# A transformer step on one core: softmax scaling and decay rows moved to other engines and queues, and a value product moved to a later stage

## The chip, the cores and the metric

The kernel runs on one core of a Trainium2 chip, as one program, once per measurement. The metric is device microseconds of one execution. TensorE (PE) does the matrix products, VectorE (DVE), ScalarE (ACT) and GpSimd (POOL) the elementwise work, and SyncE (SP) issues most of the transfers between memory and the on-chip buffers.

## The reference

One pre-norm block (a mixer with sparse attention, a cross-attention to a memory of 256 rows, a gated feed-forward part), followed by two hybrid layers. All of it is float32, with 512 positions and width 1024. The parts that the change touches:

```python
# cross-attention of the first block
kv = rmsnorm(mem, norm_mem_kv) @ w_kv_mem           # (256, 1024): keys, values
p = softmax(q @ k.T * 128 ** -0.5);  o = p @ v      # 4 heads of 128

# one of the two hybrid layers
q, k, v, z_attn, z_ssm, xbc, dt_raw = split(x @ w_in)
attn = window_attention(q, k, v, sinks) * silu(z_attn)      # 16 heads of 64, 4 key heads
xs, bm, cm = split(silu(conv4(xbc)))
dt = softplus(dt_raw + dt_bias)
a_cs = cumsum(dt * -exp(a_log))                             # inside each chunk of 128
cb = cm @ bm.T                                              # per chunk and group
y = (cb * exp(a_cs[l] - a_cs[s]) masked to s <= l) @ (xs * dt)   # 16 heads of 64
y = y + (cm @ state) * exp(a_cs) + xs * d_skip              # state carried over the chunks
ssm = rmsnorm_by_group(y * silu(z_ssm)) * ssm_norm_w
x = layer_norm(alpha * x + concat(attn, ssm) @ w_out)
```

## The kernel before

Every product with weights is made from halves: a weight tile of 128x1024 float32 is loaded (`wraw`), ScalarE casts it to a rounded half `whi`, VectorE subtracts to get `wlo` (function `weights`, three buffers of each kind), and activations are split in the same way into a pair. A product of 512 columns is then 24 matmuls of one projection: 16 with `whi` (lines L147, L148) and 8 with `wlo` (L152).

Five kinds of stage follow each other: `mem_kv` (products of the memory, and the norm of the input, in two halves A and B of 256 positions), `mixer`, `memory`, `ffn`, and twice `hybrid`. In `hybrid` the convolutions come first, then the loop over eight pairs of SSM heads, then the projections of keys (two tiles, `W[0]`, `W[1]`) and values (`W[2]`, `W[3]`), the gated norm of the second half of the heads, and the attention over (tile, key head) units, whose first work is `queries(0)`.

For a pair of heads, `decay` makes two 128x512 tiles of weights: a matmul with a selecting vector spreads a row of a_cs over the partitions (L1041), ScalarE takes Relu of the difference in four pieces (L1045) and exponents (L1047, L1048), and the tile is multiplied with `cb` (L1049), on VectorE for one head and on GpSimd for the other. `heads` uses them as operands (L1061, L1067) and VectorE combines (L1069, L1070, L1071, L1098). In the attention, VectorE and ScalarE make a softmax (L1160 to L1167), L1169 scales it, for two of four parts on GpSimd, and L1183 transposes it on TensorE.

The order on TensorE, VectorE, ScalarE and GpSimd is set by the framework's scheduler when the program is built, and each engine then works through its list in order. SP's list is the order in which the code issues, because the program asks for that:

```python
ctx.enter_context(tc.manual_schedule(engines={mybir.EngineType.SP}))
```

## Time and profile before

| | |
|---|---|
| time, median of 3 runs | 1673.09 us (1672.94 to 1673.29) |
| the profiled execution | 1672.5 us |
| its span, first to last instruction | 1670.7 us (1.8 us of the time lie around it) |
| mean granted TensorE clock over the span | 0.993 |
| busy: PE, DVE, ACT, POOL | 1621.6, 1115.1, 838.0, 239.2 us |
| share of the span | 97%, 67%, 50%, 14% |

TensorE is busy nearly all the time. A share over the whole span does not tell what ends a wait in one stage; the rows further below are taken by stage for that reason.

### The profile page before, as it was taken

Reading aid. Unit: us, or ns where it says so; the run is one execution under the profiler, and the core shown is the slowest. Engines: PE = TensorE matmul, PEld = TensorE weight load, DVE = VectorE, ACT = ScalarE, POOL = GpSimd, SP = SyncE. Lnnn points to the kernel's source line nnn. Section 1 sums busy time; section 2 is a strip of 40 time slices with the busy share of each in tenths; the row PEclk is TensorE's granted clock in tenths of the full one; section 3 lists DMA queues with packets and bytes.
Section 4 is the critical chain, followed back from the end, with each engine's and each line's share of the span. In section 5 each row is a group of like instructions: output and inputs, shape, how many; then the busy total and the mean of one; then the engine's idle time right before and its main releaser. Section 6 shows DMA issues by size and latency. Waiting matters only on the chain.

```text
span 1670.7 us, 24187 instructions
## 1 busy us (share of the span) xinstructions
PE 1621.6 (97%) x9046; PEld 1362.4 (82%) x9046; DVE 1115.1 (67%) x2199; ACT 838.0 (50%) x1648; POOL 239.2 (14%) x267
## 2 busy tenths in 40 slices
PE   8999999999999999999999999999999999999996
PEld 5778888889888888889988677777998867777786
DVE  6779866548885545523677888765487788866447
ACT  4443255336763233223554776664355477766424
POOL 2010113010200000000000223221230023222121
PEclk9999999999999999999999999999999999999998
DMA  6522322143143233234632122111452211212133
GB/s 223 196 96 76 119 96 76 64 151 119 62 150 104 89 101 101 87 102 129 212 93 89 38 64 89 64 64 56 141 177 82 79 38 57 96 61 65 66 103 112
DMA packets 57719, 166.50 MB, mean 100 GB/s; under 512 B 6673, under 2 KB 15841, under 8 KB 57601
## 3 DMA queue, kind: packets, MB, share of 16 engines
q1 hardware_dynamic: 49216, 155.21, 29.0%
q10 hardware_dynamic: 8384, 9.73, 1.8%
q8 instruction: 71, 1.16, 0.3%
q14 instruction: 48, 0.39, 0.1%
HBM read 158.61 MB, written 8.93 MB: 100 GB/s over the span
## 4 chain that ended last, share of the span: by engine, by line
PE 78%; DVE 11%; ACT 5%; issue 2%; POOL 2%; DMA 1%; SPq 0%; ACTq 0%; DVEq 0%; POOLq 0%
PE psmm L148 21%; PE psmm L152 21%; PE psmm L147 21%; DVE wlo L108 2%; POOL w L1169 2%; PE psmm L175 2%; PE psmm L173 2%; PE psmm L174 2%; ACT w L1164 1%; DVE w L1160 1%; DVE G L130 1%; PE pstr L1061 1%; PE pstr L1183 1%; PE pslg L561 1%; PE pslg L1020 1%
## 5 line engine op out<-in xcount | busy, mean ns | idle before, releaser
L147 PE MATMUL psmm<-G,whi 128*128 128x512 f32 (+1 forms) x1196 | 468.5, 393 | 1.3 <-ACT whi L107 1.3
L148 PE MATMUL psmm<-G,whi 128*128 128x512 f32 (+1 forms) x1196 | 464.3, 389 | 0.0
L108 DVE TENSOR_TENSOR wlo<-wraw,whi 128x1024 fp32r<-128x1024 f32 (+3 forms) x265 | 320.4, 1210 | 184.8 <-ACT whi L107 99.2
L107 ACT CAST whi<-wraw 128x1024 fp32r<-128x1024 f32 (+3 forms) x265 | 270.9, 1025 | 340.3 <-PE psmm L148 291.3
L152 PE MATMUL psmm<-G,wlo 128*128 128x512 f32 (+1 forms) x1196 | 296.3, 388 | 0.0
L148 PEld LDWEIGHTS psmm<-G,whi 128*128 128x128 f32 x1196 | 225.3, 188 | 47.2 <-issue 4.2
L147 PEld LDWEIGHTS psmm<-G,whi 128*128 128x128 f32 x1196 | 225.3, 188 | 47.2 <-issue 2.4
L152 PEld LDWEIGHTS psmm<-G,wlo 128*128 128x128 f32 x1196 | 222.7, 189 | 46.4 <-issue 1.5
L148 PE MATMUL psmm<-R,whi 128*128 128x256 f32 (+1 forms) x732 | 222.7, 326 | 0.0
L147 PE MATMUL psmm<-R,whi 128*128 128x256 f32 (+1 forms) x732 | 222.6, 326 | 0.0
L147 PEld LDWEIGHTS psmm<-R,whi 128*128 128x128 f32 x732 | 139.2, 190 | 11.8 <-issue 0.3
L148 PEld LDWEIGHTS psmm<-R,whi 128*128 128x128 f32 x732 | 139.2, 190 | 11.5
L152 PE MATMUL psmm<-R,wlo 128*128 128x256 f32 (+1 forms) x732 | 138.1, 326 | 0.0
L152 PEld LDWEIGHTS psmm<-R,wlo 128*128 128x128 f32 x732 | 112.8, 190 | 11.5
L198 POOL TENSOR_TENSOR acc<-acc,sq 128x512 f32<-128x512 f32 (+1 forms) x42 | 53.4, 1272 | 454.4 <-ACT sq L197 454.4
L1164 ACT ACTIVATE w<-w,st 128x256 f32<-128x256 f32 (+1 forms) x128 | 60.2, 471 | 33.5 <-DVE st L1162 33.2
L1169 POOL TENSOR_SCALAR w<-w,st 128x256 f32<-128x256 f32 x64 | 46.1, 730 | 134.6 <-DVE st L1167 127.0
L209 ACT ACTIVATE sq<-ht 128x512 f32<-128x512 f32 (+1 forms) x48 | 29.4, 613 | 58.5 <-DVE ht L907 29.3
L1049 POOL TENSOR_TENSOR R<-R,R 128x512 f32<-128x512 f32 x16 | 21.7, 1353 | 228.3 <-ACT R L1048 228.3
L907 DVE SCALAR_TENSOR_TENSOR ht<-psmm,cwh,ht 128x511 f32<-128x511 f32 (+2 forms) x72 | 53.5, 743 | 1.2
L837 DVE TENSOR_TENSOR sq<-psmm,G 128x512 f32<-128x512 f32 (+1 forms) x24 | 15.5, 645 | 57.3 <-PE psmm L152 57.3
L566 POOL TENSOR_TENSOR G<-G,G 128x384 f32<-128x384 f32 (+2 forms) x24 | 28.9, 1217 | 162.1 <-DMA G<-ts 93.4
(348 smaller groups left out, 2701.8 us busy)
## 6 DMA issues: line engine op xcount, KB each, us to landing
wraw<-w_in SPq DMA_DIRECT2D x112, 512.0 KB, 3.4
wraw<-w_out SPq DMA_DIRECT2D x56, 512.0 KB, 3.8
wraw<-w_down SPq DMA_DIRECT2D x24, 512.0 KB, 3.5
wraw<-w_gate SPq DMA_DIRECT2D x22, 512.0 KB, 3.3
wraw<-w_up SPq DMA_DIRECT2D x22, 512.0 KB, 3.3
wraw<-w_down SPq DMA_DIRECT2D x12, 384.0 KB, 3.2
wraw<-w_proj_attn SPq DMA_DIRECT2D x8, 512.0 KB, 3.4
ts<-t SPq DMA_DIRECT2D x4, 640.0 KB, 7.0
```

The costliest lines, as they stand in the source:

```text
L107: nc.scalar.copy(hi[:, :n], raw[:, :n])
L108: nc.vector.tensor_tensor(lo[:, :n], raw[:, :n], hi[:, :n].bitcast(F32), ALU.subtract)
L147: nc.tensor.matmul(out, whi[:, c], xh, start=start and k == 0, stop=False)
L148: nc.tensor.matmul(out, whi[:, c], xl, start=False, stop=False)
L152: nc.tensor.matmul(out, wlo[:, c], xh, start=False, stop=stop and k == n - 1)
L173: nc.tensor.matmul(o, whi[:, cc], xh[:, c], start=k == 0 and i % 2 == 0, stop=False, skip_group_check=True)
L174: nc.tensor.matmul(o, whi[:, cc], xl[:, c], start=False, stop=False, skip_group_check=True)
L175: nc.tensor.matmul(o, wlo[:, cc], xh[:, c], start=False, stop=k == n - 1, skip_group_check=True)
L198: (eng or nc.gpsimd).tensor_tensor(acc, acc, t, ALU.add)
L907: nc.vector.scalar_tensor_tensor(y[:, s:], pt[:, : S - s], cw(3 - s), y[:, s:], ALU.mult, ALU.add)
L1164: nc.scalar.activation(prs[b], prs[b], AF.Exp, bias=nm[:, b : b + 1], accum_out=sm[:, b : b + 1])
L1169: (nc.gpsimd if b % 2 else nc.vector).tensor_scalar(prs[b], prs[b], rc[:, b : b + 1], 1.0, ALU.mult, ALU.mult)
```

## The change

Stage 1 no longer makes the value product of the memory; the normed-by-weight memory `mgd` goes out to memory, and the stage `memory` loads it and makes the 16 products there. The memory's squares go from GpSimd to ScalarE. The first weights of `mixer` are loaded before the second half's norm. In `memory` all softmax scaling is on VectorE, the stores of `xd` go from ACT's to SP's queue, and the first three weight tiles of the next stage are split there. In `hybrid` the selecting matmuls (32 in both layers) are gone: a_cs and its exponent are written out by two transfers of ACT, and SP reads their rows back spread over the partitions (64 transfers of rows of 512 and of 384 columns). One head of a pair gets its difference on VectorE (L1045 of after, 64 pieces in both layers), the other stays on ScalarE. All products with `cb` and all softmax scaling are on VectorE. The projections of values and keys move into turns 5, 6 and 7 of the loop, and the copies of the keys' other half, eight per layer, go from GpSimd to SP. Line numbers below L133 of before shift by up to 15 in after.

```diff
     def mem_kv(self):
-        def square(k):
-            t = self.f("R")[:, :256]
-            nc.gpsimd.tensor_tensor(t if k else acc, ms[k], ms[k], ALU.mult)
-            if k:
-                nc.gpsimd.tensor_tensor(acc, acc, t, ALU.add)
...
+        for j, t in enumerate(mgs):
+            nc.sync.dma_start(self.mgd[j], t)
+        for k in range(KD):
+            self.sumsq(half(ms[k // 2])[k % 2], acc, k == 0, nc.vector)
...
-        for c in range(4):
-            w = raw(a["w_v_mem"][c])
-            for kk in range(2):
-                k = 2 * c + kk
-                for t in range(2):
-                    nc.tensor.matmul(pts[t], mg[k][:, t * P : (t + 1) * P], w[:, 512 * kk : 512 * kk + 512], start=k == 0, stop=k == 7)
...
     def memory(self):
+        def memory_values():
+            pts = [self.ps() for _ in range(2)]
+            for k in range(KD):
+                m, w = mgs[k // 2], wv[k // 2][:, S * (k % 2) : S * (k % 2) + S]
+                for t, pt in enumerate(pts):
+                    o = 256 * (k % 2) + P * t
+                    nc.tensor.matmul(pt, m[:, o : o + P], w, start=k == 0, stop=k == 7)
...
-                (nc.vector if i else nc.gpsimd).tensor_scalar(p, p, rc[:, i : i + 1], 1.0, ALU.mult, ALU.mult)
+                nc.vector.tensor_scalar(p, p, rc[:, i : i + 1], 1.0, ALU.mult, ALU.mult)
...
     def hybrid(self, L):
-        self.split(acs, ahl[0:16, :], ahl[32:48, :])
+        nc.scalar.dma_start(self.acsd[0], acs)
+        nc.scalar.activation(seg, acs, AF.Exp)
+        nc.scalar.dma_start(self.acsd[1], seg)
...
+        def decay_rows(j):
+            dfs, ee = [self.f("R") for _ in range(2)], self.f("R")
+            for e_, df in enumerate(dfs):
+                row = self.acsd[:, 2 * j + e_, :]
+                nc.sync.dma_start(df, row[:1].broadcast_to([P, S]))
+                nc.sync.dma_start(ee[64 * e_ : 64 * e_ + 64, P:], row[1:, P:].broadcast_to([64, S - P]))
+            return dfs, ee
...
         def decay(j):
+            dfs, ee = rows.pop(0)
+            if j < 6:
+                rows.append(decay_rows(j + 2))
...
-                nc.tensor.matmul(pb, self.sel[:, hd : hd + 1].broadcast_to([48, P]), ahl, start=True, stop=True)
...
-                nc.scalar.activation(ee[rows, P:], pb[rows, P:], AF.Exp)
-                nc.scalar.activation(df, df, AF.Exp, scale=-1.0)
-                (nc.vector if e_ else nc.gpsimd).tensor_tensor(df, df, cb[hd // 8], ALU.mult)
+                    if e_:
+                        nc.scalar.activation(df[:, cc], df[:, cc], AF.Relu, bias=at, scale=-1.0)
+                    else:
+                        nc.vector.tensor_scalar(df[:, cc], df[:, cc], at, 0.0, ALU.subtract, ALU.min)
+                nc.scalar.activation(df, df, AF.Exp, scale=-1.0 if e_ else 1.0)
+                nc.vector.tensor_tensor(df, df, cb[hd // 8], ALU.mult)
...
+        def keys(j):
+            pt = self.proj(W[j], h)
...
+                for t in (kh, kl):
+                    nc.sync.dma_start(t[o].bitcast(F32), t[r].bitcast(F32))
+            return ks
...
+            elif j == 5:
+                vs = token_values()
+            else:
+                kt.append(keys(j - 6))
...
-                for t in (kh, kl):
-                    nc.gpsimd.tensor_copy(t[o], t[r].bitcast(F32))
...
-                (nc.gpsimd if b % 2 else nc.vector).tensor_scalar(prs[b], prs[b], rc[:, b : b + 1], 1.0, ALU.mult, ALU.mult)
+                nc.vector.tensor_scalar(prs[b], prs[b], rc[:, b : b + 1], 1.0, ALU.mult, ALU.mult)
```

On SP, at the end of the first layer's SSM heads, before has nothing but loads of weight tiles (the third row here is the first tile of queries):

```order
L104 DMA wraw_9343<-w_in 128x1024
L104 DMA wraw_9397<-w_in 128x1024
L104 DMA wraw_9487<-w_in 128x1024
L104 DMA wraw_9557<-w_in 128x1024
L104 DMA wraw_9640<-w_in 128x1024
```

The same place in the change: 9124 and 9178 are the value tiles, 9266 is the first key tile, 9376 the second, 9473 and 9544 the first two of queries, and `G` are the halves of the split keys.

```order
L105 DMA wraw_9266<-w_in 128x1024
L1089 DMA G_9297<-G_9297 64x512
L1089 DMA G_9298<-G_9298 64x512
L1089 DMA G_9299<-G_9299 64x512
L1089 DMA G_9300<-G_9300 64x512
L105 DMA wraw_9376<-w_in 128x1024
L1089 DMA G_9407<-G_9407 64x512
L1089 DMA G_9408<-G_9408 64x512
L1089 DMA G_9409<-G_9409 64x512
L1089 DMA G_9410<-G_9410 64x512
L105 DMA wraw_9473<-w_in 128x1024
L105 DMA wraw_9544<-w_in 128x1024
```

Four copies of a key tile's halves, which need that tile's product split, now stand ahead of the load of the next tile's weights.

On TensorE, after the first key tile's product (`psmm_9272`) the change has seven matmuls of the last pair of heads (the first two and the last are shown), the sum of the gated norm's squares (L207), and the product of the second key tile (`psmm_9382`):

```order
L155 MATMUL psmm_9272<-G_6645,wlo_9269 128x512
L1058 MATMUL pstr_9419<-R_9083,G_8985 64x128
L1058 MATMUL pstr_9419<-R_9082,G_8998 64x128
...
L1058 MATMUL pstr_9419<-R_9083,G_9026 64x128
L207 MATMUL pstr_9440<-acc_9118,ones 128x512
L150 MATMUL psmm_9382<-G_6631,whi_9376 128x512
```

In before the products of both key tiles and the values stand ahead of that sum, and the queries' product follows it at once; now one key tile's product stands behind it, and the queries' (`psmm_9480`) follow that with nothing between.

On VectorE, in the first pairs of heads, before has one product with `cb` per pair (L1049, tile `R`), here beside a convolution (L907, L910) and the combining of a pair:

```order
L1070 TENSOR_TENSOR R_8649<-R_8649,pstr_8759 128x384
L1049 TENSOR_TENSOR R_8662<-R_8662,R_8397 128x512
L907 SCALAR_TENSOR_TENSOR ht_8689<-psmm_8697,cwh_7787,ht_8689 128x511
L1069 SCALAR_TENSOR_TENSOR G_8353<-G_8353,vecs,pstr_8750 128x512
L907 SCALAR_TENSOR_TENSOR ht_8689<-psmm_8697,cwh_7787,ht_8689 128x510
L1071 TENSOR_TENSOR G_8353<-G_8353,R_8649 128x384
```

The change has there, with the difference in pieces (L1045) and two products (L1047) per pair:

```order
L1045 TENSOR_SCALAR R_8684<-R_8684,dtt_8304 128x128
L1133 TENSOR_TENSOR G_8315<-G_8315,R_7825 128x512
L1045 TENSOR_SCALAR R_8684<-R_8684,dtt_8304 128x128 x3
L1047 TENSOR_TENSOR R_8685<-R_8685,R_8399 128x512
L1045 TENSOR_SCALAR R_8743<-R_8743,dtt_8304 128x128 x4
L111 TENSOR_TENSOR wlo_8785<-wraw_8782,whi_8784 128x1024
L1047 TENSOR_TENSOR R_8684<-R_8684,R_8399 128x512
L1047 TENSOR_TENSOR R_8743<-R_8743,R_8399 128x512
```

Four pieces and a second product per pair of heads are added to VectorE's list between the combining of one pair and the weights of the next projection.

## Rows read from the trace of the kernel before

**Rows 1.** Busy time of each engine in stretches of the span, in us.

```profile
core 0: us, PE busy (x) PEld busy (x) DVE busy (x) ACT busy (x) POOL busy (x), PEclk, DMA share, GB/s
0.00:20.00 20.00, 13.73 (x52) 10.75 (x53) 11.36 (x23) 4.82 (x10) 11.23 (x20) 1.00 0.92 304
399.60:494.40 94.80, 87.85 (x671) 83.95 (x672) 78.18 (x198) 66.38 (x172) 10.25 (x14) 0.96 0.25 84
920.90:991.80 70.90, 69.66 (x376) 49.08 (x375) 60.11 (x85) 54.55 (x124) 16.38 (x12) 1.00 0.17 53
1030.00:1154.20 124.20, 120.81 (x698) 97.25 (x697) 85.83 (x254) 80.29 (x219) 28.90 (x46) 1.00 0.19 61
```

**Rows 2.** What TensorE waited for: line, releaser, total us, times, longest.

```profile
PE pstr L1183 <- POOL w L1169: 5.7, 14, 0.6
PE pslg L1154 <- DVE G L130: 5.0, 2, 2.5
PE pstr L204 <- DVE acc L198: 4.4, 2, 3.4
```

**Rows 3.** The value product of the memory in stage 1, by line and shape.

```profile
L710 PE MATMUL pslg<-wraw,R 128*128 128x512 f32 x32 | 14.5, 595 | 0.0
```

**Rows 4.** TensorE in order of time, at four places of the first layer.

```profile
931.00 0.49 PE L1041 MATMUL pslg<-ahl,selr 48*128 48x512 f32 x1
931.43 0.50 PE L152 MATMUL psmm<-G,wlo 128*128 128x512 f32 x1
...
1012.97 0.28 PE L1127 MATMUL psmm<-whi,G 128*128 128x256 f32 x1
1013.09 0.28 PE L1128 MATMUL psmm<-wlo,G 128*128 128x256 f32 x1
...
1020.13 0.39 PE L147 MATMUL psmm<-G,whi 128*128 128x512 f32 x1
1020.35 0.39 PE L148 MATMUL psmm<-G,whi 128*128 128x512 f32 x1
...
1025.08 0.33 PE L1154 MATMUL pslg<-G,G 128*128 128x128 f32 x1 [2.52 <-DVE G L130]
```

**Rows 5.** VectorE's groups by shape, 932.9 to 1024.8 us.

```profile
L1098 DVE TENSOR_TENSOR G<-G,R 128x512 f32<-128x512 f32 x8 | 8.4, 1056 | 0.1
L1071 DVE TENSOR_TENSOR G<-G,R 128x384 f32<-128x384 f32 x8 | 6.8, 846 | 0.1
```

**Rows 6.** VectorE in order of time, first layer.

```profile
938.67 0.69 DVE L1098 TENSOR_TENSOR G<-G,R 128x512 f32<-128x512 f32 x1
...
1022.49 1.22 DVE L108 TENSOR_TENSOR wlo<-wraw,whi 128x1024 fp32r<-128x1024 f32 x1
...
1024.34 0.68 DVE L130 TENSOR_TENSOR G<-psmm,G 64x512 fp32r<-64x512 f32 x1
```

**Rows 7.** VectorE's nearest kind to the new pieces, whole span, by shape.

```profile
L453 DVE TENSOR_SCALAR G<-G,st 128x128 f32<-128x128 f32 x8 | 2.2, 281 | 0.0
```

**Rows 8.** GpSimd's products with `cb`, 932.9 to 1024.8 us.

```profile
L1049 POOL TENSOR_TENSOR R<-R,R 128x512 f32<-128x512 f32 x7 | 9.4, 1341 | 33.7 <-ACT R L1048 33.7
```

**Rows 9.** ScalarE in order of time, end of the first layer's heads.

```profile
1015.08 1.28 ACT L220 ACT_TABLE_LOAD   x1
...
1019.58 1.04 ACT L107 CAST whi<-wraw 128x1024 fp32r<-128x1024 f32 x1
...
1022.46 0.57 ACT L129 CAST G<-psmm 64x512 fp32r<-64x512 f32 x1
```

**Rows 10.** SP's loads of a layer's weights: KB each, median us from issue to landing.

```profile
wraw<-w_in SPq DMA_DIRECT2D x112, 512.0 KB, 3.4
```

**Rows 11.** What SP's queue waited for: total us, times, longest.

```profile
SPq L104 <- DVE wlo L108: 1241.9, 218, 30.9
```

**Rows 12.** The stretches behind TensorE's two longest waits; PEclk is the granted clock.

```profile
466.40:473.20 6.80, 6.26 (x24) 5.47 (x25) 5.20 (x9) 5.14 (x9) 0.00 (x0) 0.51 0.51 147
1026.10:1029.50 3.40, 3.40 (x11) 2.68 (x10) 3.34 (x9) 2.18 (x3) 0.00 (x0) 0.54 0.09 36
```

More of the change, by code (lines that the diff above doesn't have):

```diff
@@ L457, in mixer @@
         h = self.h
-        W = iter(range(32))
+        W = iter(range(2, 32))
         unit = lambda: self.proj(a["w_in"][next(W)], h)
-        first = [(self.ps(), 68, self.weights(a["w_idx"], 8 * 68))]
-        first += [(self.ps(), P, self.weights(a["w_in"][next(W)])) for _ in range(2)]
+        first = [(self.ps(), m, w) for m, w in self.first]
         for c in self.HALVES:
@@ L672, in mem_kv @@
         for k in range(KD):
-            t = self.f("R")[:, :256]
-            nc.vector.tensor_scalar(t, ms[k], self.col("norm_mem_kv", k), None, ALU.mult)
+            m, t = half(ms[k // 2])[k % 2], half(mgs[k // 2])[k % 2]
+            nc.vector.tensor_scalar(t, m, self.col("norm_mem_kv", k), None, ALU.mult)
             mg.append(t)
-            square(k)
+        banks = [self.ps("lg") for _ in range(2)]
+        pks = [t for bank in banks for t in half(bank)]
         for j in range(4):
-            if j == 3:
-                wk.append(raw(a["w_k_mem"][3]))
-                self.consts2()
-            pt = self.ps()[:, :256]
-            pks.append(pt)
             for k in range(KD):
-                nc.tensor.matmul(pt, wk[j][:, k * P : k * P + P], mg[k], start=k == 0, stop=k == 7)
-        self.bias_tables()
+                nc.tensor.matmul(pks[j], wk[j][:, k * P : k * P + P], mg[k], start=k == 0 and j % 2 == 0, stop=k == 7,
+                                 skip_group_check=True)
         self.h = self.pairs("G")
@@ L689, in mem_kv @@
         self.pump()
+        self.first = [(68, self.weights(a["w_idx"], 8 * 68))] + [(P, self.weights(a["w_in"][j])) for j in range(2)]
+        self.consts2()
+        for j, t in enumerate(mgs):
+            nc.sync.dma_start(self.mgd[j], t)
+        for k in range(KD):
+            self.sumsq(half(ms[k // 2])[k % 2], acc, k == 0, nc.vector)
         self.rstd(rs, acc, 1e-6)
-        rt = self.s("rt", (P, 4), 2)[:, :2]
+        self.rtm = self.s("rtm", (P, 2))
         pr = self.ps("tr")
@@ L694, in mem_kv @@
             nc.tensor.matmul(pr[:, t : t + 1], acc[:, t * P : (t + 1) * P], self.ones[:, :1], start=True, stop=True)
-        self.inv_sqrt(rt, pr[:, :2], self.s("ru", (P, 2), 2), 1e-6)
-        def key(j):
+        self.inv_sqrt(self.rtm, pr[:, :2], self.s("ru", (P, 2), 2), 1e-6)
+        self.pending = norm(B)
+        self.pump(1)
+        for j in range(4):
             t = self.f("ht")[:, :256]
@@ L809, in memory @@
                 pb.append(logits(j, B))
+        self.ahead = [self.weights(z) for z in (a["w_gate"][0], a["w_up"][0], a["w_gate"][1])]
         for j in range(4):
@@ L844, in ffn @@
         g = [self.f("ht") for _ in range(2)]
-        first = [self.weights(z) for z in (a["w_gate"][0], a["w_up"][0], a["w_gate"][1])]
-        first.append(self.held(a["w_up"][1], "R"))
+        first = self.ahead + [self.held(a["w_up"][1], "R")]
         for c in self.HALVES:
@@ L1207, in queries @@
             return qs
+        self.piece = S
         q = queries(0)
```

152 lines of the change are left out of this document (67 added, 85 removed).

## The prediction, made before the changed kernel was run

> **What bounds the kernel now.** I read the shares by stretch first. TensorE is the bound nearly everywhere: in the first layer's SSM heads it works 69.7 of 70.9 us, and VectorE 60.1 of the same 70.9 [rows 1]. So VectorE has about 11 us of room there, no more. Then the list of waits: in the attention it is GpSimd's half of the softmax scaling that ends 14 short waits, 5.7 us in both layers; where a layer passes from heads to attention, the split of the first queries ends a wait of 2.5 us, twice; and a sum of squares ends one of 3.4 us in the memory stage [rows 2]. Behind two such gaps the clock is lower: after the 3.4 us gap, 6.8 us at 0.51 of full speed, after the 2.5 us gap, 3.4 us at 0.54 [rows 12], which is the 1.2 GHz level instead of 2.4, so that about half of each stretch is lost. The first 20 us hold 6.3 us without TensorE work [rows 1].
>
> **Stage 1 and the memory stage.** Stage 1 loses 32 records of the value product, 14.5 us busy [rows 3]. That work stands in a stage with idle TensorE time, ahead of the second half's norm. What VectorE and ScalarE do for this norm stays, and they now also square the memory. So not all of it is gained: at most about 11 us, at least 3, if the norm is what ends last. I take 6.5, a little under half of the 14.5, since I see nothing left that TensorE could do in the wait for that norm. The same product costs its 14.5 us in the memory stage, but that stage has 94.8 − 87.9 = 6.9 us without TensorE work and a lower clock after its longest gap, worth 3.4 us [rows 1, 12]. The product's matmuls stand among the logits and the next stage's first three weight tiles are split early, so most of these 10.3 us can be covered. Cost: between 14.5 − 10.3 = +4.2 and +8 if the gap at the sum of squares stays whole; below, +1 if the order saves switches as well. I take +4. The xd transfers that go to SP's list stand ahead of loads that are needed later than they arrive; I cost them at nothing, hidden by the 94.8 us stage, and up to 2 us if that cover is gone.
>
> **Heads: VectorE's list.** Per layer 16 selecting matmuls go. One takes 0.43 us from its start to the next matmul's [rows 4], and the switches around it some more, so about 8 us of TensorE work. But VectorE gains work in the same stretch: 32 pieces of 128x128, 0.28 each by the nearest row [rows 7], and eight products, 0.69 each by a row of the same shape [rows 6]. That is 14.5 us by durations; neighbours overlap a little, so I take 12 (bounds 10 and 14.5). What it gets back is GpSimd's disturbance: L1098 takes 1.06 on the mean and 0.69 undisturbed, eight times, and L1071 0.85 against about 0.55 [rows 5, 6]: 5.4 us at most, 4.5 taken, because GpSimd keeps the sums of squares. The split of the second value weights now also stands in this list, 1.2 us [rows 6]. Sum: 60.1 + 12 + 1.2 − 4.5 = 68.8 us, and VectorE can't have these weights ready before 920.9 + 68.8 = 989.7; the first value weights 1.8 us earlier. From 987.9 TensorE then has 96 matmuls at 0.12 and 24 at 0.22 [rows 4], 11.5 + 5.4, and ends the first key product at T = 1005. Its own work alone would let it be there earlier: before, it ended values and both key products at 1013.3; less 1.2 of waits, 8 of selecting matmuls, 5.4 and 0.9 for the second key product and seven small matmuls that now come after T, 998. So VectorE, with 69 us in its list, becomes the bound of the heads and costs 7 us of the 8 that were saved.
>
> The Trainium skill's page GPSIMD Engine Reference, section Engine selection, sends elementwise work with two inputs to VectorE, since GpSimd takes about twice as long. The trace agrees: 1.34 us on GpSimd [rows 8], 0.69 on VectorE [rows 6]. By that rule alone each moved product is a gain, and T would be 998; by the count of VectorE's list it is 1005.
>
> **From heads to attention: SP's list.** SP keeps its order, and every wait in it holds what stands behind: 1241.9 us of the span its loads wait for a buffer [rows 11]. Now four copies that need the split of a key tile stand ahead of the next weights. After T: two casts of 0.57 [rows 9] and two subtractions of 0.68 [rows 6], one after the other with one combining instruction of the last pair between, 2.9 us with hand-offs; then the load, 3.4 to landing [rows 10]; the cast of its first half, 1.04 [rows 9]; hand-offs 0.5. The second key product starts at T + 7.9. TensorE has 1.4 us for that time (seven small matmuls and the sum). It ends at T + 13.3. Meanwhile the gated norm's chain, which waits in ScalarE's list behind that cast, takes 4.5 us on ScalarE (from 1015.08 to 1019.58 before) [rows 9], and 4 more of VectorE; so the split of the second keys is done only at about T + 19.4 and the queries' weights are ready at T + 24.3. If that chain held nothing up, at T + 21.2. Work in these 24.3 us is 6.8, so 17.5 us are idle (14.4 at best), where before one gap of 2.5 us stood. Behind such gaps I expect the lower clock: 2.5 us lost in all (1.7 as behind 2.5 us of gap, up to 5 if both are like the one behind 3.4) [rows 12]. The first logits come after the queries' product and seven matmuls of the next, 7.0 us: 1005 + 24.3 + 7.0 + 2.5 = 1038.8. Before they come at 1025.1 [rows 4], with 1.7 lost to the clock behind it and five more matmuls done, 1.1: 1025.7 alike. Cost: 13.1 us per layer.
>
> The Trainium skill's page Trainium Kernel Development and Optimization, section Key Constraints, says that issuing transfers from several engines saves only issue time. By that, the move of the copies to SP's list would cost no more than eight issues, and the 13 us would not be there; that is a rival below. Against it its page DMA: Bandwidth & Descriptors, section Anatomy of one DMA, puts a transfer's wait on the issuing sequencer, and the trace agrees with the latter: SP waits 1241.9 us in 218 waits [rows 11].
>
> **Attention.** GpSimd's two scalings of four go to VectorE, which has 124.2 − 85.8 = 38 us of room in that stage [rows 1]. The 14 waits go: 2.9 us per layer by the row [rows 2], with the restart of TensorE about 4 (bounds 2 and 5).
>
> **Sum.** 2 × (13.1 − 4.0) = +18.2, stage 1 −6.5, memory +4: +15.7 on the profiled 1672.5, 1688.2. The median of the runs shown is 0.6 above that execution, so 1688.8; I say 1688.
>
> **Rivals.**
> - *SP's loads are not held* (faster). Were the next weights loaded in spite of the waiting copies, the second key product and the queries would follow at once, T + 6.8: 17.5 + 2.5 less per layer, 1688 − 40 = 1648. For it speaks only that the loads are small beside the stage; against it that SP's list is in order [rows 11] and that the rows of order show no load ahead. It decides the sign: with less than about 10 us of idle time per layer instead of 17.5, the change is faster. Chance 0.13, with the cases between.
> - *VectorE keeps up in the heads.* If the pieces and products cost the lower bound and the disturbance goes whole, T is 998 and the kernel 14 us shorter: 1674, no change. For it: GpSimd's rest is short; against it: VectorE's room was 11 us and the list wants 9 more, with its own waits. Chance 0.17.
> - *More waits.* VectorE's list waits for ScalarE and TensorE in between, 2 us per layer; both gaps bring the long clock stretch, 2.5 more per layer; stage 1 gains 3: 1688 + 9 + 3.5, about 1700. Chance 0.2.
>
> **How the numbers follow.** My forecast has 0.5 and its own range 1680 to 1695. To hold 8 in 10 the range goes from 1668, which takes in most of the second rival, to 1701. About 0.2%, 3.3 us, is what a measurement of this kernel can tell from no change. Faster (below 1669.7): the first rival and a part of the second, 0.18. Same (to 1676.4): most of the second, 0.12. Slower: 0.70.
>
> **What would show it.** In the profile of the changed kernel: two idle stretches of TensorE, 5 to 9 us each, behind the first and the second key product in each layer, ended by the cast of a weight tile, with SP waiting in a copy just before; a PEclk near half behind them; VectorE over 9 tenths busy in the heads, and TensorE waiting there for VectorE's weights; no waits of L1189 (L1183 before) for a scaling by GpSimd; a first stage 3 to 11 us shorter and a memory stage 1 to 8 us longer. The prediction is wrong if the key products follow each other without a gap, or if TensorE is still fully busy in the heads.

## The result and the profile after

The changed kernel takes 1731.94 us (median of 4 runs, 1731.34 to 1732.62) where the kernel before takes 1673.01 us beside it: 1.0353 times as long, 95% interval 1.0335 to 1.0371. That is 59 us more; the forecast was 15 us more, and its range ended at 1701. The profiled span is 1729.5 us at a mean granted clock of 0.974.

First the shares by stretch, as in [rows 1]: the first 20 us, the memory stage, the first layer's heads up to the end of the first key product, the transition to the first queries and logits, and the attention.

```profile
core 0: us, PE busy (x) PEld busy (x) DVE busy (x) ACT busy (x) POOL busy (x), PEclk, DMA share, GB/s
0.00:20.00 20.00, 14.81 (x57) 12.62 (x58) 8.85 (x30) 8.44 (x20) 0.62 (x5) 1.00 0.86 285
393.70:502.70 109.00, 101.37 (x705) 89.76 (x705) 82.73 (x210) 68.92 (x177) 5.07 (x6) 0.97 0.24 77
942.00:1026.10 84.10, 73.56 (x428) 58.99 (x430) 64.65 (x114) 43.54 (x78) 7.02 (x5) 0.92 0.16 49
1026.10:1059.90 33.80, 19.37 (x71) 14.06 (x71) 18.23 (x27) 15.70 (x20) 1.66 (x2) 0.75 0.48 140
1059.90:1186.90 127.00, 126.11 (x722) 101.75 (x721) 92.23 (x306) 80.57 (x221) 9.65 (x14) 1.00 0.19 63
```

In the heads TensorE is idle for 10.5 of 84.1 us, and the granted clock is 0.92 in the mean; VectorE is busy for 64.65: under 8 tenths, where I had written over 9. So both engines have room, and yet the stretch is longer. In the transition TensorE works 19.4 of 33.8 us.

What TensorE waited for, as in [rows 2] (total us, times, longest):

```profile
PE psmm L150 <- ACT whi L108: 25.5, 7, 9.7
PE pstr L1058 <- DVE R L1047: 13.7, 6, 4.3
PE pstr L207 <- POOL acc L201: 10.3, 2, 5.1
PE pstr L207 <- DVE acc L201: 6.6, 3, 4.1
```

The waits for GpSimd's scaling and for the queries' split, the first two of [rows 2], are gone from the top. In their place stand a cast of weights (L108), the decay tiles' product with `cb` (L1047, new) and the sum of the second norm. The same in order of time, TensorE at the heads' start and behind the two key products:

```profile
938.65 1.29 PE L155 MATMUL psmm<-G,wlo 128*128 128x512 f32 x5
942.29 0.63 PE L1058 MATMUL pstr<-R,G 128*64 128x128 f32 x2 [2.34 <-DVE R L1047]
...
1026.02 1.09 PE L1058 MATMUL pstr<-R,G 128*64 128x128 f32 x14
1032.24 2.07 PE L207 MATMUL pstr<-acc,ones 128*128 128x512 f32 x2 [5.14 <-POOL acc L201]
...
1040.16 1.52 PE L155 MATMUL psmm<-G,wlo 128*128 128x512 f32 x6
1050.97 0.80 PE L150 MATMUL psmm<-G,whi 128*128 128x512 f32 x1 [9.29 <-ACT whi L108]
```

And SP's queue in that time, its issues:

```profile
993.48 0.33 SPq L105 DMA_DIRECT2D wraw<-w_in  x1
1026.74 2.60 SPq L1089 DMA_DIRECT2D G<-G  x4
1029.43 0.54 SPq L105 DMA_DIRECT2D wraw<-w_in  x1
1042.85 3.33 SPq L1089 DMA_DIRECT2D G<-G  x4
1046.24 1.07 SPq L105 DMA_DIRECT2D wraw<-w_in  x2
```

What SP's copies waited for between 900 and 1060 us (total, times, longest):

```profile
SPq L1089 <- ACT G L135: 45.8, 2, 32.9
```

From 993.5 to 1026.7 SP issues nothing: it stands in the first key copy until ScalarE has cast the key tile. The load of the next weights goes out at 1029.4, behind the four copies, and the same happens again at 1042.9. The two idle stretches of 5.1 and 9.3 us stand where the forecast put them. The second is ended by the cast of a weight tile, as forecast, the first by GpSimd's part of the norm's sum (L201); the next weights, loaded at 1029.4, were cast only at 1034.2, so TensorE would have waited for them to about that time without the sum.

The longest wait in the heads, 4.3 us, ends in a product with `cb`, and that product in an exponent of ScalarE. What ScalarE did before it, and TensorE's wait:

```profile
997.18 1.28 ACT L227 ACT_TABLE_LOAD   x1
998.47 1.28 ACT L212 ACT_TABLE_LOAD   x1
1000.38 1.28 ACT L229 ACT_TABLE_LOAD   x1
1002.58 1.28 ACT L1046 ACT_TABLE_LOAD   x1
1003.88 0.63 ACT L1046 ACTIVATE R<-R 128x512 f32<-128x512 f32 x1
...
1005.38 0.66 PE L1058 MATMUL pstr<-R,G 128*64 128x128 f32 x2 [4.26 <-DVE R L1047]
```

Ahead of the exponent (L1046) ScalarE makes part of the first gated norm (L229) and the next projection's silu (L212), and changes its function table four times, 1.28 us each. The kernel before makes four such loads in its loop too (982.5 to 996.4), and there TensorE waits 0.8 us at most; the runs e5 and e13 below make one. No run changes this alone.

The stages of the first layer and of the block ahead, from the first matmul of one to the first of the next (worked out from the traces; "heads" runs from the first product for `cb` to the first logits), in us, with the experiments below:

| kernel | time | first stage | memory | heads | attention |
|---|---|---|---|---|---|
| before | 1673.0 | 55.2 | 101.5 | 127.6 | 129.4 |
| after | 1731.9 | 50.4 | 115.7 | 154.7 | 127.0 |
| e1 keys' copies on GpSimd | 1700.7 | 48.8 | 114.7 | 135.4 | 130.4 |
| e2 and keys, values behind the loop | 1700.1 | 49.9 | 115.2 | 138.8 | 129.5 |
| e3 rows from TensorE | 1691.0 | 51.1 | 115.8 | 135.9 | 127.1 |
| e4 no splits ahead | 1734.2 | 50.0 | 115.3 | 157.4 | 127.1 |
| e5 e1 and e3 | 1671.9 | 50.9 | 114.5 | 121.8 | 131.0 |
| e6 memory part alone | 1679.4 | 50.6 | 114.7 | 127.6 | 128.7 |
| e7 e1, pieces on ScalarE | 1706.5 | 48.8 | 114.8 | 139.8 | 130.4 |
| e8 e5, memory as before | 1663.6 | 54.6 | 101.6 | 121.8 | 130.7 |
| e9 e1, heads in turn | 1727.4 | 50.0 | 114.5 | 147.4 | 133.2 |
| e10 e9, memory as before | 1718.9 | 55.6 | 102.1 | 147.8 | 131.9 |
| e11 attention scale alone | 1670.3 | 55.3 | 101.7 | 127.5 | 127.8 |
| e12 copies behind the loads | 1701.3 | 49.1 | 114.8 | 136.0 | 130.7 |
| e13 e9, casts ahead of decay | 1666.9 | 49.0 | 115.1 | 124.7 | 125.7 |
| e14 e13, memory as before | 1660.4 | 56.3 | 102.1 | 125.0 | 125.7 |
| e15 half the value product | 1725.7 | 50.9 | 108.1 | 156.6 | 127.1 |

The second layer does the same within 3 us (after: 156.1 and 127.0). The first stage differs by up to 2.3 us between kernels that are alike there.

### The profile page after: what moved, and what is told of

Same layout as the page of the kernel before. It is cut to its first block, busy times and chain, and to the rows that moved or that the text cites. A ratio compares the mean times of both kernels' runs of the same rounds, so it can differ in the third digit from the quotient of the medians.

```text
span 1729.5 us, 24153 instructions
## 1 busy us (share of the span) xinstructions
PE 1633.0 (94%) x9014; PEld 1375.0 (80%) x9014; DVE 1133.7 (66%) x2388; ACT 812.3 (47%) x1563; POOL 138.7 (8%) x148
## 4 chain that ended last, share of the span: by engine, by line
PE 82%; DVE 10%; ACT 4%; DMA 2%; issue 1%; SPq 0%; DVEq 0%; ACTq 0%
PE psmm L150 22%; PE psmm L151 21%; PE psmm L155 21%; PE pstr L1189 1%; PE psmm L178 1%; PE psmm L176 1%; PE psmm L177 1%; PE psmm L1204 1%; DMA wraw<-w_in 1%; DVE wlo L111 1%; ACT w L1170 1%; PE psmm L725 1%; PE pslg L562 1%; PE pslg L1160 1%; PE pstr L1058 1%
## 5 line engine op out<-in xcount | busy, mean ns | idle before, releaser
L108 ACT CAST whi<-wraw 128x1024 fp32r<-128x1024 f32 (+3 forms) x262 | 267.3, 1023 | 347.5 <-PE psmm L151 285.4
L150 PEld LDWEIGHTS psmm<-G,whi 128*128 128x128 f32 x1196 | 229.3, 192 | 78.2 <-ACT whi L108 31.2
L151 PEld LDWEIGHTS psmm<-G,whi 128*128 128x128 f32 x1196 | 229.1, 192 | 45.3 <-issue 0.8
L151 PE MATMUL psmm<-R,whi 128*128 128x256 f32 (+1 forms) x684 | 210.6, 329 | 0.0
L150 PE MATMUL psmm<-R,whi 128*128 128x256 f32 (+1 forms) x684 | 210.4, 329 | 0.0
L150 PEld LDWEIGHTS psmm<-R,whi 128*128 128x128 f32 x684 | 130.0, 190 | 11.8 <-issue 0.3
L151 PEld LDWEIGHTS psmm<-R,whi 128*128 128x128 f32 x684 | 130.0, 190 | 11.5
L155 PE MATMUL psmm<-R,wlo 128*128 128x256 f32 (+1 forms) x684 | 130.4, 329 | 0.0
L201 POOL TENSOR_TENSOR acc<-acc,sq 128x512 f32<-128x512 f32 (+1 forms) x42 | 51.9, 1235 | 818.3 <-ACT sq L200 818.3
L155 PEld LDWEIGHTS psmm<-R,wlo 128*128 128x128 f32 x684 | 106.2, 190 | 11.5
L212 ACT ACTIVATE sq<-ht 128x512 f32<-128x512 f32 (+1 forms) x48 | 29.4, 613 | 67.7 <-DVE ht L893 38.4
L200 ACT ACTIVATE sq<-G 128x256 f32<-128x256 f32 (+1 forms) x76 | 34.8, 462 | 42.6 <-DVE G L1133 19.5
L1166 DVE CUSTOM_DVE_ANT_0 w<-pslg,w,sinks 128x256 f32<-128x256 f32 (+1 forms) x128 | 51.1, 446 | 0.3
L1148 POOL TENSOR_SCALAR w<-dist 128x256 f32<-128x256 f32 x32 | 21.8, 680 | 321.7 <-PE pstr L1189 265.4
```

What stands on the lines that cost most here:

```text
L108: nc.scalar.copy(hi[:, :n], raw[:, :n])
L150: nc.tensor.matmul(out, whi[:, c], xh, start=start and k == 0, stop=False)
L151: nc.tensor.matmul(out, whi[:, c], xl, start=False, stop=False)
L155: nc.tensor.matmul(out, wlo[:, c], xh, start=False, stop=stop and k == n - 1)
L200: self.last_sq = nc.scalar.activation(t, src, AF.Square)
L201: (eng or nc.gpsimd).tensor_tensor(acc, acc, t, ALU.add)
```

## The experiments

### Where the transition's time went

**e1: the keys' copies on GpSimd.**

```diff
-                    nc.sync.dma_start(t[o].bitcast(F32), t[r].bitcast(F32))
+                    nc.gpsimd.tensor_copy(t[o], t[r].bitcast(F32))
```

> The changed kernel with the sixteen copies of the keys back on GpSimd instead of SP's queue. Theory A (SP's queue stands behind those copies, and the weights of the second key product and of the first queries behind SP): the idle stretches of 5.1 and 9.3 us behind the two key products go, and the half clock behind them, so 15 to 20 us per layer and 30 to 40 in all, to about 1697 us. The program's order also puts the sum of the second norm behind the second key product then, which A needs. Rival B (the chain of the second norm on ScalarE and VectorE holds the casts of the next weights as long as SP does): less than 8 us per layer, and a time above 1716 us, with a TensorE wait of 5 us or more left in that place.

Measured: 1700.66 us, ratio to before 1.0168 (1.0152 to 1.0185): 31.3 us less than the changed kernel. The heads are 19.3 us shorter and the attention 3.4 longer. Of the two idle stretches a wait of 0.9 us for the sum is left. This is what theory A asked for, but the scheduler also moved the norm's sum behind the queries' product here, so by itself the run doesn't tell the queue from that order.

**e12: the copies behind the loads.** The copies stay with SP and only change places in its list; TensorE's list is again the scheduler's.

```diff
-                for t in (kh, kl):
-                    nc.sync.dma_start(t[o].bitcast(F32), t[r].bitcast(F32))
+                late.extend((t, r, o) for t in (kh, kl))
...
         q = queries(0)
+        for t_, r, o in late:
+            nc.sync.dma_start(t_[o].bitcast(F32), t_[r].bitcast(F32))
```

> The changed kernel with the keys' copies still by SP, but in SP's list behind the loads of the weights of the second key product and of the first queries; nothing else. If the loads' place behind the copies is the cost (SP waits in a copy for the key's halves and issues no load meanwhile), it comes near the run with the copies on GpSimd: 1698 to 1708 us. If the copies' own transfers, landing late for the first logits or taking the transfer engines, are the cost: 1720 to 1732 us.

Measured: 1701.30 us, ratio 1.0173 (1.0157 to 1.0188), the same as e1. SP in that stretch:

```profile
1006.68 2.06 SPq L105 DMA_DIRECT2D wraw<-w_in  x2
1025.52 8.00 SPq L1218 DMA_DIRECT2D G<-G  x8
1033.57 1.54 SPq L105 DMA_DIRECT2D wraw<-w_in  x3
```

Both loads now go out at 1006.7, some 19 us before the first copy can start. The eight copies themselves cost nothing that can be seen, so the 15 us per layer are not the transfers. The norm's sum stands behind the queries' product here too, as in e1, so neither run has the loads early and the sum in its old place. The trace of the changed kernel tells the two apart as far as it goes: both casts that the second key product and the queries needed waited for their own load (ScalarE idle 2.3 and 4.3 us for it, up to 1033.1 and 1049.9), and each load had been issued behind four copies. So SP's held loads bound both products, and the sum's place in the list is at most a part of the first stretch. The Trainium skill's page DMA: Bandwidth & Descriptors, section Anatomy of one DMA — SWDGE (gpsimd) path, puts a transfer's wait on the sequencer that issues it. The 32.9 us in which SP stood in one copy agree.

### Where the heads' time went

**e2: keys and values behind the loop again**, with the copies on GpSimd; the two convolutions that the change had put ahead of the loop go back into it.

```diff
-            elif j == 5:
-                vs = token_values()
-            else:
-                kt.append(keys(j - 6))
...
+        kt += [keys(0), keys(1)]
+        vs = token_values()
         gated_norm(1, accs[1])
```

> The changed kernel with the keys' copies on GpSimd, and with the key and value products behind the loop over the heads again, as in the kernel before; the rows of the decay stay with SP's transfers. If where the key and value products stand costs nothing by itself, the time is that of the run with the copies alone, within 5 us. If the products inside the loop are what fills TensorE's waits there, the loop gets longer without them and the time is 8 to 20 us above that run. If they crowd the loop's lists and hold the decay's pieces back, it is 8 to 20 us below it, near 1680 us.

Measured: 1700.08 us, ratio 1.0164 (1.0145 to 1.0184). Where these products stand makes no difference while the rows come by SP.

**e3: the rows from TensorE again.** Selecting matmuls, all pieces on ScalarE, the products with `cb` shared with GpSimd; copies and order as changed.

```diff
-            dfs, ee = rows.pop(0)
+                nc.tensor.matmul(pb, self.sel[:, hd : hd + 1].broadcast_to([48, P]), ahl, start=True, stop=True)
...
-                nc.vector.tensor_tensor(df, df, cb[hd // 8], ALU.mult)
+                (nc.vector if e_ else nc.gpsimd).tensor_tensor(df, df, cb[hd // 8], ALU.mult)
```

> The changed kernel with the decay rows from TensorE again: the selector products, all eight pieces of a pair on ScalarE, the masks' products shared by GpSimd and VectorE; the keys' copies and the order of the products stay as changed. TensorE has 6.6 us more work per layer. Theory A (the rows' new route costs the heads the 13 us per layer by which they are longer than forecast, since each pair's pieces stand in VectorE's list behind products that wait for TensorE): 5 to 10 us per layer are won back, about 1712 to 1722 us. Rival C (VectorE's list is not the cause, and the order of the key and value products is): no gain, 1732 us or up to 13 us more.

Measured: 1691.03 us, ratio 1.0115 (1.0096 to 1.0133): 40.9 us less, two to four times what I expected, although TensorE does more work. So what goes with the rows' new route is the largest single cost of the change; the edit also moves the pieces and the products with `cb`, which e7 tests. With the copies on GpSimd the same edit is worth 28.8 us (e1 against e5 below). In the loop of the first layer no wait of TensorE is over 1.5 us; one of 8.6 us for a weight cast is left in the transition, since SP still holds the copies.

**e5: e1 and e3 together.**

> The two edits of the second and third kind together: decay rows from TensorE and the keys' copies on GpSimd, the rest as changed. If the two costs lie in different places (the copies' in the transition, the rows' in the loop over the heads), what each wins alone adds up: 1731.9 less 31.3 less 40.9, about 1660 us. If part of the rows' cost is the transition itself (in the run with TensorE's rows one idle stretch of 8.6 us is left there instead of two of 5.1 and 9.3 us), only that stretch and the half clock behind it remain to be won, 10 to 13 us per layer: 1665 to 1671 us. Rival: the copies meet the masks' products on GpSimd and hold the second norm's sum: 1680 us or more.

Measured: 1671.94 us, ratio 0.9992 (0.9983 to 1.0002): no change against before. It is 12 us above the plain sum of the two gains and just above the second reading (1665 to 1671), by which a part of the transition was won by both. The first layer's heads, in two parts:

```profile
906.10:947.50 41.40, 41.40 (x194) 32.60 (x192) 32.95 (x45) 19.53 (x35) 1.30 (x1) 1.00 0.23 77
947.50:1027.90 80.40, 78.24 (x493) 62.20 (x491) 62.31 (x88) 56.55 (x124) 23.31 (x20) 1.00 0.16 53
```

TensorE works 119.6 of 121.8 us, and the heads are 5.8 us shorter than before, the attention 1.6 us longer: with TensorE's rows, keys and values inside the loop are a gain of some 4 us per layer, of which the softmax scale has a part (e11).

**e7: e1 with all pieces on ScalarE**, and the products with `cb` shared with GpSimd; the rows still by SP.

```diff
-                        nc.vector.tensor_scalar(df[:, cc], df[:, cc], at, 0.0, ALU.subtract, ALU.min)
+                        nc.scalar.activation(df[:, cc], df[:, cc], AF.Relu, bias=at, scale=-1.0)
```

> As the run with the keys' copies on GpSimd (1700.7 us), with the rows still by SP's transfers, but all eight pieces of a pair on ScalarE and the masks' products shared by GpSimd and VectorE as in the kernel before. If VectorE's list is what holds the heads (the pieces stand behind products that wait for TensorE, and so the next pair's decay is late), TensorE's waits of 2.3, 4.3 and some 1 us for the masks' products in the loop go and 8 to 12 us per layer are won: 1676 to 1685 us. If it is the rows' way through device memory and SP's queue, those waits stay: 1694 to 1702 us.

Measured: 1706.50 us, ratio 1.0200 (1.0185 to 1.0216), 6 us more than e1. The reading that VectorE's added pieces are the cost is wrong. TensorE now waits 6.8 us for the products of VectorE and 6.7 for those of GpSimd, so the waits were there whoever made the tile. The other reading, the rows' way through memory, is not shown either: no wait of TensorE, ScalarE or VectorE for a row's landing stands among the long ones.

**e9: e1 with the heads in turn.** In e1 pairs of heads stand back to back in TensorE's list, as in the changed kernel at 942.3. Here each pair is put behind the projection of its own turn.

```diff
+            last = [i for i in nc.cur_bb.bb.instructions if i.engine == mybir.EngineType.PE][-1]
             nxt = decay(j + 1) if j < 7 else None
...
-            heads(j, *ws)
+            with self.tc.issue_after(last):
+                heads(j, *ws)
```

> As the run with the keys' copies on GpSimd (1700.7 us), the rows still by SP's transfers and half of the pieces on VectorE; only TensorE's list is changed: the products of each pair of heads stand behind the projection of their own turn, so that one projection lies between two pairs, as it does with TensorE's rows (there a pair's rows could not be made before the bank of the last pair was free, and the heads of 80 us had no wait over 0.5 us). Theory D (with the rows there early, pairs bunch in TensorE's list, at 939, 941 and 944 us and again at 956, 985 and 995 us, and each waits for its mask's product with nothing behind which to hide): the waits of 2.3, 1.0, 1.0 and 4.3 us for the masks' products and the half clock behind them go, 12 to 20 us per layer: 1660 to 1677 us. Rival (the pieces on VectorE or the rows' landing are late whatever the list): 1690 to 1702 us.

Measured: 1727.42 us, ratio 1.0325 (1.0308 to 1.0343): 27 us slower than e1, where 24 to 41 faster was expected. Theory D is wrong as it stood: the waits for the products with `cb` went, and longer ones came, for weight casts. TensorE at the first of them:

```profile
939.05 0.84 PE L155 MATMUL psmm<-G,wlo 128*128 128x512 f32 x3
947.12 0.79 PE L150 MATMUL psmm<-G,whi 128*128 128x512 f32 x1 [7.22 <-ACT whi L108]
```

ScalarE ahead of that cast:

```profile
940.61 0.62 ACT L1046 ACTIVATE R<-R 128x512 f32<-128x512 f32 x1
...
941.71 0.62 ACT L1046 ACTIVATE R<-R 128x512 f32<-128x512 f32 x1
942.23 0.97 ACT L1043 ACTIVATE R<-R,dtt 128x128 f32<-128x128 f32 x3
943.24 0.63 ACT L1046 ACTIVATE R<-R 128x512 f32<-128x512 f32 x1
...
944.62 0.63 ACT L1046 ACTIVATE R<-R 128x512 f32<-128x512 f32 x1
945.16 0.97 ACT L1043 ACTIVATE R<-R,dtt 128x128 f32<-128x128 f32 x3
946.04 1.03 ACT L108 CAST whi<-wraw 128x1024 fp32r<-128x1024 f32 x1
```

SP's last load of weights before it, and the next one:

```profile
920.33 0.34 SPq L105 DMA_DIRECT2D wraw<-w_in  x1
...
948.54 0.34 SPq L105 DMA_DIRECT2D wraw<-w_in  x1
```

No weight load goes out between 920.3 and 948.5, and a load takes 3 to 4 us to land, so the tile that is cast at 946.0 had been on the chip for about 20 us. Ahead of its cast ScalarE made exponents (L1046) for two pairs of heads and pieces (L1043) of a third, while the first pair's matmuls came only at 955. The decays run two pairs ahead, because their rows are there, and the weights that TensorE needs first stand behind them. In the next such wait, 5.1 us up to 969.7, a row is late as well: its transfer goes out only at 963.8, when the first pairs' matmuls have freed its buffer, lands 3 us later, and the cast stands behind its exponent.

**e13: the casts ahead of the decay.** e9, and each turn's weights are loaded and split before the next pair's decay is issued, on ScalarE and VectorE. No work is added or removed. TensorE's list is close to that of e9; one projection and the first matmuls of the values come a turn earlier. In SP's list each load of weights moves ahead of the rows that stood before it.

```diff
+        def paced(j):
+            w = [self.weights(u) for u in units[j]]
+            with self.tc.issue_after(end(E.Activation)), self.tc.issue_after(end(E.DVE)):
+                return w, decay(j)
...
-            nxt = decay(j + 1) if j < 7 else None
+            w, nxt = paced(j + 1) if j < 7 else (None, None)
```

> As the run with the heads in turn (1727.4 us), and besides, each turn's weights are loaded and split ahead of the next pair's decay in ScalarE's and VectorE's lists: the decay's instructions stand behind the cast and the subtraction of the projection that follows. Theory E (with the rows there early, the decays of two pairs ahead crowd ScalarE's and VectorE's lists, and what stands behind them is late: masks' products in one order of TensorE's list, weight casts in the other, where TensorE waited 7.2, 5.1, 4.3 and 5.1 us for them): those waits go and the heads get as short as with TensorE's rows or shorter, 14 to 20 us per layer: 1687 to 1700 us, and down to 1665 us if the loop has no wait left. Rival F (ScalarE and VectorE simply have too much to do in the loop with these rows): the waits change their names and the time stays at 1715 us or more.

Measured: 1666.85 us, ratio 0.9969 (0.9957 to 0.9981): 60.6 us less than e9 and 33.8 less than e1. The loop of the first layer:

```profile
950.60:1028.20 77.60, 75.65 (x488) 62.07 (x487) 67.24 (x118) 44.64 (x79) 15.86 (x15) 1.00 0.27 93
```

TensorE works 75.7 of 77.6 us, and VectorE does 67.2 us of work beside it. Just ahead of this stretch one wait for a cast is left in each layer:

```profile
943.14 0.80 PE L150 MATMUL psmm<-G,whi 128*128 128x512 f32 x1 [4.88 <-ACT whi L108]
```

So theory E holds for the loop but for this wait: with the same work the order of the lists makes 60.6 us. The first wait of e9 was due to ScalarE's order, since its tile had lain ready for 20 us; how much of the rest SP's new order has is not told apart, and the casts first without the heads in turn were not run. Rival F, too much work there, is refuted, and the forecast's step on VectorE with it.

### The memory part

**e4: no splits ahead.**

```diff
-        self.ahead = [self.weights(z) for z in (a["w_gate"][0], a["w_up"][0], a["w_gate"][1])]
...
-        first = self.ahead + [self.held(a["w_up"][1], "R")]
+        first = [self.weights(z) for z in (a["w_gate"][0], a["w_up"][0], a["w_gate"][1])]
```

> The changed kernel with the first three weights of the feed-forward stage split in that stage again, not ahead of the last value products of the memory stage. Theory (the three casts of 1.0 us and three subtractions of 1.2 us stand ahead of the transposed probabilities' copies in ScalarE's and VectorE's lists): the TensorE waits of 2.1 and 1.2 us in the memory stage go, 2 to 5 us are won there, and up to 2 us lost at the start of the feed-forward stage: 1727 to 1731 us. Rival (the memory stage is longer by its value product and the slow clock alone): within 1 us of 1732, or above it.

Measured: 1734.15 us, ratio 1.0363 (1.0343 to 1.0383), no gain. The two waits went from 2.1 and 1.2 us to 0.4 and 0.3, but others came later in the stage (2.3 us for the second half's sum, 1.4 for a cast), and the stage stayed at 115 us. The splits only move the wait.

**e6: the memory part alone**, on the kernel before.

> The kernel before with the change in the first stage and the memory stage alone (the memory's value product moved, the mixed weights split ahead, the normed memory kept in device memory, the copies of x by SP). If these parts are what the stage table says, 4.8 us less in the first stage and 14.2 us more in the memory stage: 1680 to 1683 us. Rival: part of the 14.2 us comes from the softmax scale on VectorE, which is not in this kernel: 1674 to 1679 us.

Measured: 1679.40 us, ratio 1.0041 (1.0027 to 1.0056), 6.5 us slower, between the two readings. The first stage gives 4.6 and the memory stage takes 13.2, so the softmax scale, which is not in this kernel, has at most 1 us of the 14.2.

**e15: half of the value product left out**, so that the values are only half summed.

```diff
-            for k in range(KD):
+            for k in range(4):
```

> The changed kernel with half of the memory's value product left out (four of the eight blocks of the contraction, 16 of 32 passes of 0.43 us, so the values are only half summed). If the moved product covers none of the memory stage's waits and is all added to TensorE's list, 6.9 us less: 1724 to 1726 us, all of it in the memory stage. If it fills waits that open again without it, as my forecast took it to, 0 to 3 us less: 1729 us or more.

Measured: 1725.72 us, ratio 1.0313 (1.0295 to 1.0330), 6.2 us less; the memory stage is 7.6 us shorter for 16 passes less, 6.9 us of work. The waits of that stage before and behind the missing work are the same. TensorE in the changed kernel and then in this one:

```profile
451.40 0.67 PE L207 MATMUL pstr<-acc,ones 128*128 128x256 f32 x2 [1.29 <-DVE acc L201]
454.16 0.56 PE L769 MATMUL psmm<-ht,G 128*128 128x256 f32 x1 [2.09 <-ACT ht L132]
455.91 0.58 PE L770 MATMUL psmm<-sq,G 128*128 128x256 f32 x1 [1.19 <-DVE sq L133]
```

```profile
445.39 0.67 PE L207 MATMUL pstr<-acc,ones 128*128 128x256 f32 x2 [1.29 <-DVE acc L201]
448.15 0.39 PE L769 MATMUL psmm<-ht,G 128*128 128x256 f32 x1 [2.09 <-ACT ht L132]
449.91 0.58 PE L770 MATMUL psmm<-sq,G 128*128 128x256 f32 x1 [1.36 <-DVE sq L133]
```

The moved product stands at 400 to 418 us, where TensorE is busy throughout (18.00 of 18.00 us), and the waits come at 450 to 478. It covers none of them.

### What is worth keeping

**e11: the attention's softmax scale alone**, on the kernel before.

```diff
-                (nc.gpsimd if b % 2 else nc.vector).tensor_scalar(prs[b], prs[b], rc[:, b : b + 1], 1.0, ALU.mult, ALU.mult)
+                nc.vector.tensor_scalar(prs[b], prs[b], rc[:, b : b + 1], 1.0, ALU.mult, ALU.mult)
```

> The kernel before with one edit, the attention's softmax scale on VectorE for all four blocks. If the 2.2 us per layer by which the attention is shorter with the change come from this edit: 1668 to 1670 us. If they come from the split of the queries' weights in halves or from the keys' place: 1672 to 1674 us.

Measured: 1670.25 us, ratio 0.9986 (0.9977 to 0.9996): 2 to 3 us, a small gain of its own. The profile has 1.6 and 1.0 us less in the two attentions; the rest of the changed kernel's 2.3 and 2.0 is not told apart.

**e8: e5 with the first stage and the memory stage as before.**

> Decay rows from TensorE, the keys' copies on GpSimd, the first stage and the memory stage as in the kernel before; what is left of the change is the softmax scales on VectorE and the key and value products inside the loop over the heads. 9 us less than the run with TensorE's rows and the copies on GpSimd: by the sum 1651 us, by the other reading 1656 to 1662 us. If the key and value products in the loop gain nothing, only the scales' 4 us are left: 1668 us.

Measured: 1663.62 us, ratio 0.9946 (0.9931 to 0.9961): 8.3 us less than e5, just above the second reading (1656 to 1662), and 4 us under the 1668 of the scales alone.

**e10: e9 with these two stages as before.**

> The run with the heads in turn, with the first stage and the memory stage as in the kernel before. The memory part cost 8.3 us between the two runs with TensorE's rows: the time of the run with the heads in turn less 8 us; by theory D 1652 to 1669 us, and below 1663.6 us if the 6.6 us per layer that TensorE no longer spends on the rows are a gain once the pairs stand in turn.

Measured: 1718.91 us, ratio 1.0277 (1.0262 to 1.0292): 8.5 us less than e9 for the memory part, as from e5 to e8 (8.3); the rest fell with e9.

**e14: e13 with these two stages as before.**

> The run with the casts before the decay, with the first stage and the memory stage as in the kernel before: 8 to 9 us less than that run. By theory E 1656 to 1692 us; it beats the 1663.6 us of the mix with TensorE's rows only if the loop has no wait left.

Measured: 1660.36 us, ratio 0.9929 (0.9913 to 0.9946), the fastest here and 12.1 us under the kernel before as run beside it (1672.45). That is some 3 us under e8, with TensorE's rows, though TensorE is spared 16 matmuls of 0.43 us in each layer. It does not show that SP's rows are the better ones: the heads are 3.2 us longer than e8's and the attention 5.0 shorter, and TensorE's rows with the order of e13 were not run.

## Why the prediction was wrong

The direction was right (0.70 for slower), the size was not: 59 us instead of 15. Two steps failed, the time of the heads and the cover in the memory stage. Term by term, from the stages of both profiles:

| term | forecast | measured |
|---|---|---|
| first stage | −6.5 | −4.8 |
| memory stage | +4 | +14.2 |
| heads and transition, per layer | +13.1 | +27.1 and +28.2 |
| attention, per layer | −4 | −2.3 and −2.0 |

**Right: from heads to attention.** From the end T of the first key product to the queries' product I had 24.3 us; in the trace it is 1026.1 to 1051.0, 24.9, and 33.8 to the first logits, as in my sum (24.3 + 7.0 + 2.5). The idle stretches (5.1 and 9.3 us, 5 to 9 forecast) and SP waiting in the copies are as described; of their ends only the second is (above). Idle are 14.4 us, not 17.5, and some 4.8 us went to the half clock, not 2.5, so that two errors nearly cancel in the 33.8. e1 and e12 show that the whole is worth 15 us per layer, and e12 that it needs nothing but another place in SP's list. The first rival (SP's loads are not held) is refuted. By the rule that issuing from several engines saves only issue time (the Trainium skill, Trainium Kernel Development and Optimization, section Key Constraints) the copies would have cost their issues alone. Measured were 31 us for sixteen copies, which made the loads behind them wait.

**Wrong: "VectorE's list", T = 1005.** The changed kernel comes to the heads 7.95 us later than the one before (905.24 against 897.29), so its T of 1026.1 is 1018.2 on the time scale of before: 13 us late, and 14.5 in the second layer by the same count, nearly all that is missing. It is not SP's: in e1 and e12, without the held loads, the way from the heads' start to T is as long (120.6 and 120.4 us; 120.6 in the changed kernel). In e5 it is 99.5 and in e13 101.7, with one pair's 1.9 us of matmuls less ahead of T; my 998 for TensorE's own work alone is 100.5 on this count.

I had summed VectorE's work to 68.8 us and let the sum decide. It didn't: VectorE was busy for less than 8 tenths of the stretch, and in e13 it did 67.2 us of work beside a TensorE that worked 75.7 of 77.6. What took the time was the order. In the 84.1 us up to T TensorE is idle for 10.5 us and does 12.0 us of its work at half clock, which is some 6 us more (rows in the last section); I had put the waits that end so, and the clock in the heads, at nothing. With rows that lie ready, the scheduler put the decays of two pairs ahead of the weight casts, and TensorE waited for a product or for a cast, whichever stood behind (e1, e9). At the longest wait, 4.3 us, the exponent itself stood behind the first norm and its table loads. That e13 mends most of this with the same work shows that it is the order. That the selecting matmuls, for all their 0.43 us each, had paced the decays before is my reading of it: a pair's rows were made on TensorE between two projections, so its decay came when it was needed, as in e5. The sum of an engine's list bounds a stretch from below; I used it as the time. The order was mended only with the copies on GpSimd (e13); the changed kernel with SP's copies and this order was not run.

**Wrong: the memory stage, +4.** The step that failed is "most of these 10.3 us can be covered". The work is nearly as priced, 32 passes of 0.43, 13.8 us for 14.5, and all of it was added (e15, e6), 14.2 us in the stage: idle time in a stage covers work only where the work stands in the list at the time of the wait. The early splits, which I had counted among the cover, changed nothing (e4).

**Half right: first stage and attention.** The first stage gained 4.8 of 14.5 us (between 3 and 11, 6.5 taken). The attention gained half of what was forecast, at its lower bound.

The rival *More waits*, 1700 us, had the right mechanism, waits in turn between the engines in the heads, at 2 us per layer instead of 13. The rival *VectorE keeps up* is what the loop of e13 shows, only that it needs another order.

## What to carry to other kernels

Before a wait or an instruction is taken out of a list, ask what it paced: work that became ready early was put early here, and in lists that are worked through in order it delays what is needed first. On a queue that is worked in order, put a transfer that waits for a computation behind the loads that wait for nothing; swapping the two was worth 31 us here without any other edit. Idle time seen in a stage counts as cover only for work that can stand in the list where the wait is.

## What the runs showed of the hardware

The clock was a larger part of the loss than I had priced. Behind the waits in the heads and around the two before the second key product and the queries, TensorE runs at the lower of its levels (1.2 GHz), also where it is busy all the time; the changed kernel, first layer, granted clock in the column behind GpSimd's:

```profile
942.30:945.70 3.40, 3.40 (x20) 2.85 (x21) 3.40 (x8) 3.37 (x10) 0.00 (x0) 0.50 0.00 0
966.20:969.60 3.40, 3.40 (x9) 2.65 (x8) 3.40 (x6) 1.15 (x2) 1.27 (x1) 0.50 0.00 0
1003.80:1010.60 6.80, 5.22 (x22) 4.76 (x23) 4.67 (x7) 6.78 (x13) 0.00 (x0) 0.50 0.01 2
1010.60:1013.00 2.40, 2.40 (x22) 2.40 (x21) 2.37 (x3) 0.00 (x0) 1.68 (x1) 1.00 0.00 0
...
1031.10:1037.90 6.80, 5.66 (x11) 3.41 (x12) 1.82 (x2) 4.71 (x5) 1.49 (x2) 0.50 0.18 61
1044.70:1054.90 10.20, 3.93 (x9) 3.18 (x10) 5.62 (x10) 4.01 (x5) 0.00 (x0) 0.50 0.79 245
```

TensorE is busy for 12.0 us at 0.50 in the heads and for 9.6 in the transition. An estimate by half of that is 6 and 4.8 us lost, on top of the waits themselves; in the kernel before it is 1.7 in the same place. In the stretches of e5 and e13 shown above the granted clock is 1.00; behind the 4.9 us that are left in e13 it is 0.50 for 3.1 us (942.9 to 946.0).
